# Second layer's first MLP product: four more f tiles as seven half-size products

## The chip, the cores and the metric

The kernel runs on one core of a Trainium2 chip. The metric is the time of one execution on the device, in microseconds (us); lower is better. All times here are of single-core runs of the whole program.

## What is computed

A decoder of two layers on one sequence of 512 tokens of 1024 columns, all in float32. The first layer mixes tokens by pooling windows, the second by a gated unit; each is followed by a norm, a modulation and an MLP with a squared ReLU. The change lies in the MLP of the second layer alone. Cut to that, the reference reads:

```python
def sq_relu_mlp(h, w1, w2):
    return jnp.square(jax.nn.relu(h @ w1)) @ w2

# for each layer i
h = modulate(rmsnorm(x, norm_mlp_g[i]), sh2, sc2)
x = x + g2[:, None, :] * sq_relu_mlp(h, mlp_w1[i], mlp_w2[i])
```

Here `h` is 512 x 1024, `mlp_w1[i]` is 1024 x 4096 and `mlp_w2[i]` is 4096 x 1024. The product with `w1` is called M1, the one with `w2` M2.

## The kernel before

**Three products for one.** Each float32 operand is split in two rounded parts, `h` and `l` ("high" and "low"): `split(r)` lets ACT copy the tile into `wh` (line 167) and DVE subtract it into `wl` (line 168); `parts(o, a)` does the same for activations (lines 592, 593). `mm3` (lines 176 to 178) then issues three matmuls for each product: `wl` by `h`, `wh` by `l`, `wh` by `h`. `H(k, c)` is the pair of parts of the normed activations (tile `hb`), for 128 input columns `k` and tokens `c`; `h32` holds the same values unsplit.

**M1 of the second layer.** The 4096 columns of `w1` are 32 tiles of 128, called f tiles; they are numbered in four chunks `c` of eight, and each chunk is two groups `j` of four. The result of a group is one tile `g[c, j]`.

- Tiles 0 to 3 of chunk 0 are made by `first1`: for each half of the tokens, four tiles of 8 times 3 matmuls of 256 columns. Between the halves the second half of the norm (`normed(1, 1, 1)`) runs, and `spill(1)` sends x out to memory.
- Tiles 4 to 7 of chunk 0 are the units `("f", (0, f))`: `f_prep` loads one weight tile (`w1f`, 512 KB) and splits it, `f_run` issues 2 x 8 x 3 = 48 matmuls of 256 columns, and `put` has ACT do the ReLU (line 630) and the square (line 618).
- Chunks 1 to 3 are units `("s", (c, j, m))`. A group of four f tiles by all the input columns is treated as a 2 x 2 block product and done as seven half-size products `m` after Winograd's scheme, in the order 1, 5, 6, 3, 7, 2, 4. Each has 2 x 4 x 3 = 24 matmuls of 256 columns. `s_prep` makes the weights of a product, `s_run` issues the matmuls and puts the results together: products 1, 6 and 5 are copied from the bank by ACT (line 742), 2, 3 and 7 are combined by DVE (lines 745, 747, 749), and each of the four blocks gets its ReLU (line 750) and its square.

**The weights of an s unit.** The four blocks `b(r, n)` of a group are loaded from `w1b` (512 KB each, SP queue, line 155) into the pool `w4`, which has three buffers. Block (0,0) is product 1's weight as it is; DVE then adds block (0,1) to it for product 5 and block (1,1) for product 6 (line 706), and after product 6's split a DMA on the POOL queue adds block (1,0) from memory for product 4 (line 701). A second such DMA adds block (1,1) to block (0,1) for product 7. Products 3 and 2 use blocks (1,1) and (1,0) as they are. Five pairs of `wh`, `wl` buffers (pool `wts`) let preparation run up to five units ahead of the matmuls.

**The activations of an s unit.** `a_sums(step)` makes the four operands that are sums, in steps 0 to 3 for products 5, 6, 3 and 7, out of `h32`, in place: one, one, two and no DVE operations of 128 x 1024 elements (lines 667 and 680 among them), and a `parts` each (one ACT, one DVE operation). Their results go to the tile of `hx`, to the buffers of `x0` and `x1` (free once x has been spilled), and to `H(slice(0, 4), half)`, over the activations that only plain products read. It is called after each of the four f units.

**The order of work.** TensorE (PE) runs in the order written. The other engines' instructions and the DMA issues are put in order when the program is built, by dependence and priority, and each engine then takes its queue in that order. M2 units `("p", (c, m))` follow from chunk 1 on, mixed with s units. `spread_cols(gain, dg)` (four matmuls, line 216) stands after the last unit of chunk 0.

Of the kernel before, what the change touches and what calls it, by code (L numbers as in the profile page):

```python
# [10 lines left out]
ALU = mybir.AluOpType  # L11
# [3 lines left out]
P = 128  # L15
D = 1024
# [29 lines left out]
def c_g(n, k):  # L46
    return 24 * n + 16 + k
# [31 lines left out]
def decoder_kernel(ctx: ExitStack, tc: tile.TileContext, xtok, vecs, rows, fgrow, ada0, adag, ada1, pool_w, w1s, w1, w1f, w1b, w2, w2e, w_v, w_u, w_o, wsT, lnp, bs, out):  # L79
    nc = tc.nc  # L80
    V, A, G, T = nc.vector, nc.scalar, nc.gpsimd, nc.tensor
# [13 lines left out]
    def shift(pool, words):  # L95

        if words % LINE:
            pool.tile([P, words % LINE], F32, name="shift", tag=f"shift{len(shifts)}", bufs=1)
            shifts.append(words)
# [6 lines left out]
    def bank(name, pool=None):  # L106
        pool = pool or ps
        return pool.tile([P, S], F32, name=name, tag="mm" if pool is ps else "xz")
# [33 lines left out]
    def H(k, c):  # L142

        return h_[0][:, 0, k, c], h_[0][:, 1, k, c]
# [8 lines left out]
    def raw4(src):  # L153
        r = w4.tile([P, D], F32, name="raw", tag="w4")
        nc.sync.dma_start(r, src)
        return r
# [7 lines left out]
    def split(r):  # L164

        h, l = wpair()
        A.activation(h, r, AF.Copy)  # L167
        V.tensor_tensor(l, r, f32(h), ALU.subtract)  # L168
        return h, l
# [35 lines left out]
    def diagonals(dg, cols):  # L205
        for k in range(KD):
            G.tensor_scalar(dg[:, k], ident, cols[:, k : k + 1], None, ALU.mult)

    def spread_cols(cols, dg=None):

        if dg is None:
            dg = w4.tile([P, KD, P], F32, name="dg", tag="w4")
            diagonals(dg, cols)
        for n in range(2):
            po = bank("pb")
            T.matmul(po, ones, dg[:, 4 * n : 4 * n + 4], start=True, stop=True)  # L216
            A.activation(gb[:, S * n : S * n + S], po, AF.Copy)
# [15 lines left out]
    with (  # L233
# [14 lines left out]
        m = band.rearrange("p n g w -> p (n g) w")  # L248
        G.affine_select(out=m, in_=m, compare_op=ALU.is_ge, fill=0.0, base=0, pattern=[[0, 8], [1, W]], channel_multiplier=-1)
        for g in range(4):  # L250
            m = band[:, :, g]
# [284 lines left out]
        for op in WORK.split():  # L536
            on_v, op = op.endswith("V"), op.rstrip("V")
            kind, d = op.rstrip("0123456789"), [int(c) for c in op if c.isdigit()]
# [51 lines left out]
    def parts(o, a):  # L590

        A.activation(o[0], a, AF.Copy)
        V.tensor_tensor(o[1], a, f32(o[0]), ALU.subtract)

    def mlp(i, first, extra, last, ending):
# [3 lines left out]
        with (  # L599
# [56 lines left out]
            def a_sums(step):  # L656


                def a(r, j):
                    return h32[0][:, 4 * j : 4 * j + 4, 256 * r : 256 * r + 256]  # L660

                def operand(pool, tag):
                    t = pool.tile([P, 2, 4, 256], F32R, name="as", tag=tag)
                    return t[:, 0], t[:, 1]

                def minus(o, p, q):
                    V.tensor_tensor(o, p, q, ALU.subtract)

                first, half = slice(0, 256), slice(256, 512)
                if step == 0:  # L670
                    sums_a.update({1: H(slice(0, 4), first), 2: H(slice(4, 8), first), 4: H(slice(4, 8), half)})
                    shift(hx, LINE - GAP)
                    minus(a(1, 1), a(1, 0), a(1, 1))
                    m, o = 5, operand(hx, "hx")
                elif step == 1:
                    minus(a(1, 1), a(1, 1), a(0, 0))
                    m, o = 6, operand(big, "x0")
                elif step == 2:
                    minus(a(0, 0), a(0, 0), a(1, 0))
                    V.tensor_tensor(a(1, 1), a(1, 1), a(0, 1), ALU.add)  # L680
                    m, o = 3, operand(big, "x1")
                else:
                    m, o = 7, H(slice(0, 4), half)
                parts(o, a(0, 0) if m == 7 else a(1, 1))
                sums_a[m] = o

            blks = {}

            def blk(c, j, r, n):
                if (c, j, r, n) not in blks:  # L690
                    blks[c, j, r, n] = raw4(w1b[2 * (c - 1) + j, r, n])
                return blks[c, j, r, n]

            def s_prep(u):
                c, j, m = u

                def b(r, n):
                    return blk(c, j, r, n)

                def add(o, r, n):  # L700
                    G.dma_start(o, w1b[2 * (c - 1) + j, r, n], accum_op=ALU.add)


                t = b(0, 0)
                if m in (5, 6):
                    V.tensor_tensor(t, t, b(*CHAIN[m]), ALU.add)
                if m == 5:
                    add(b(0, 1), 1, 1)
                wb = b(1, 1) if m == 3 else b(1, 0) if m == 2 else b(0, 1) if m == 7 else t
                w = split(wb)  # L710
                if m == 6:
                    add(t, *CHAIN[4])

                nxt = (c, j + 1) if j == 0 else (c + 1, 0)
                more = {1: (c, j, 0, 1), 5: (c, j, 1, 1), 3: (c, j, 1, 0), 7: (*nxt, 0, 0), 2: (*nxt, 0, 1), 4: (*nxt, 1, 1)}.get(m)
                if more and more[0] < 4:
                    blk(*more)
                return w
# [182 lines left out]
            gain = mods[i][:, c_g(1, 0) : c_g(1, 0) + KD]  # L901
            done = first(put)
            if i:
                dg = su.tile([P, KD, P], F32, name="dgu", tag="u")
                diagonals(dg, gain)
            units = [("f", (0, f)) for f in range(done, 8)]
            for c in range(3):
                if i == 0:
                    fs, lead, step = [("f", (c + 1, f)) for f in range(8)], 3, (1,) * 7
# [31 lines left out]
            for n, (kind, u) in enumerate(units):  # L941
                for m in range(n, ahead(n)):
                    if m not in ready:
                        ready[m] = prep[units[m][0]](units[m][1])
                while at < len(extra) and at < due * (n + 1):
                    extra[at]()
                    at += 1
                run[kind](u, ready[n])
                if i and kind == "f":
                    a_sums(u[1] - 4)  # L950
                    if u == (0, 7):
                        spread_cols(gain, dg)
                if i and u == (3, 1, 4):
                    reload()

# [77 lines left out]
    with (  # L1033
# [27 lines left out]
        for t in range(NT):  # L1061
# [6 lines left out]
            r = rsqrt(ag[:, 1:2], 1.0, LN_EPS, 1)  # L1068
# [4 lines left out]
        u, gt, wu = {}, {}, {}  # L1073
# [79 lines left out]
    def last1(t, c0, n, src, y):  # L1153
# [13 lines left out]
        else:  # L1167
# [5 lines left out]
            nc.sync.dma_start(out[t, :, 1], X(t)[:, S:D])  # L1173

    mlp(1, first1, [], last1, lambda: None)


# [11 lines left out]
def _lay_out(inp):  # L1189
    import numpy as np  # L1190

    def f(name):
        return np.asarray(inp[name], dtype=np.float32)

    def cols(v):
        return v.reshape(-1, P).T

    def fmajor(w, ct):

        return w.reshape(KD, P, -1, ct).transpose(2, 1, 0, 3).reshape(-1, P, KD * ct)  # L1200

    def halves(w):

        return w.reshape(4, 2, P, 2, S).transpose(3, 0, 2, 1, 4)

    order = _ada_columns()
    d = {}
    d["xtok"] = f("x")[0].reshape(NT, P, D)
    adab = f("ada_b").reshape(2, 48, P)[:, order]
    d["vecs"] = np.concatenate([cols(v) for v in (f("c"), adab, f("norm_mix_g"), f("norm_mlp_g"))], axis=1)  # L1210
    d["rows"] = np.stack([f("c")[0], adab[0, 16:24].reshape(-1), f("pool_scale")[0]])
    d["fgrow"] = f("final_g")
    aw = f("ada_w").reshape(2, D, 48, P)[:, :, order]

    v0 = aw[0].transpose(1, 2, 0)
    d["ada0"] = np.concatenate([v0[0:16], v0[24:40]] + [v0[16 + 2 * g : 18 + 2 * g] for g in GT])
    d["adag"] = aw[0][:, 16:24].reshape(2, 4, P, 4, 256).transpose(3, 0, 2, 1, 4)[GM]
    d["ada1"] = np.concatenate([v0[40:48], aw[1].transpose(1, 2, 0)])
    d["pool_w"] = f("pool_w")[0].reshape(8, P, 256).transpose(1, 0, 2)
    w1 = f("mlp_w1")  # L1220
    d["w1s"] = w1[0].reshape(KD, P, -1)[:, :, 0 : P * SWEEP]
    d["w1"] = fmajor(w1[0], P)
    d["w1f"] = fmajor(w1[1][:, :D], P)

    d["w1b"] = w1[1][:, D:].reshape(2, 4, P, 6, 2, 256).transpose(3, 0, 4, 2, 1, 5).reshape(6, 2, 2, P, D)

    w2 = f("mlp_w2").reshape(2, 4, 2, 4, P, 2, S)
    d["w2"] = w2[:, 0:3].transpose(0, 1, 2, 5, 4, 3, 6)
    d["w2e"] = np.stack([halves(w[3 * D :]) for w in f("mlp_w2")])
    win = f("sgu_w_in")[0]  # L1230
    d["w_v"] = halves(win[:, D:])
    d["w_u"] = fmajor(win[:, :D], P)
    d["w_o"] = halves(f("sgu_w_out")[0])
    d["wsT"] = f("sgu_w_s")[0].transpose(2, 0, 1)
    d["lnp"] = np.concatenate([f("sgu_ln_g")[0], f("sgu_ln_b")[0]])
    d["bs"] = f("sgu_b_s")[0].reshape(-1)
    return {k: np.ascontiguousarray(v) for k, v in d.items()}
# [17 lines left out]
```

## Time and profile before

| | us |
|---|---|
| median of 3 runs | 873.24 |
| lowest and highest | 872.81, 873.34 |
| the profiled execution, its own time | 873.16 |
| its span in the profile | 871.5 |
| granted TensorE clock, mean | 0.997 of full |

| engine | busy us | share of the span |
|---|---|---|
| TensorE matmul (PE) | 861.0 | 99% |
| weight load (PEld) | 741.6 | 85% |
| VectorE (DVE) | 670.1 | 77% |
| ScalarE (ACT) | 451.3 | 52% |
| GpSimd (POOL) | 66.9 | 8% |

Matmuls are pipelined: each is shown with its own length (0.28 us for 256 columns), but the next one starts well before it ends, so what a matmul costs is the distance from one start to the next. In the timeline a row gives the start, the length, the engine, the line, the operation, what is written and read, and in brackets the idle time of the engine just before it with what ended that.

### The profile page before, as it was taken

What the parts mean: (1) busy time and instruction counts of PE and PEld (TensorE: products, weight loads), DVE (VectorE), ACT (ScalarE), POOL (GpSimd) and SP (SyncE); (2) the same over time, 40 slices, a digit from 0 to 9 for tenths busy, and PEclk for the clock granted to TensorE, in tenths of its full rate; (3) what the DMA queues carried; (4) which work ended last, traced back from release to release, by engine and by line L of the source; (5) the groups of instructions that cost most, each with busy time, mean ns of one, the idle gap of its engine ahead of it and who ended that gap; (6) DMA issues with size and microseconds to landing.
All of it is one profiled execution on the core that took longest, in us unless ns stands there. A gap on an engine that the chain in (4) does not pass through costs nothing.

```text
span 871.5 us, 11804 instructions
## 1 busy us (share of the span) xinstructions
PE 861.0 (99%) x4580; PEld 741.6 (85%) x4580; DVE 670.1 (77%) x881; ACT 451.3 (52%) x653; POOL 66.9 (8%) x87
## 2 busy tenths in 40 slices
PE   9999999999999999999999999999999999999996
PEld 7878888788888888888878888999999998999885
DVE  6889696779869886657798866667777698679755
ACT  4285755554444445237333326666765576566521
POOL 3000003000000000000410012000101000100001
PEclk9999999999999999999999999999999999999998
DMA  9969853553554341615548525937758587677302
GB/s 350 417 229 311 274 193 137 193 193 121 181 204 169 128 162 51 215 37 205 193 155 288 185 73 222 319 87 179 171 193 178 156 225 224 136 162 261 123 24 97
DMA packets 39517, 161.80 MB, mean 186 GB/s; under 512 B 4387, under 2 KB 4515, under 8 KB 34214
## 3 DMA queue, kind: packets, MB, share of 16 engines
q1 hardware_dynamic: 35282, 137.72, 44.0%
q0 software_dynamic: 4032, 23.07, 13.0%
q8 instruction: 36, 0.59, 0.3%
q10 hardware_dynamic: 148, 0.27, 0.1%
q14 instruction: 19, 0.16, 0.1%
HBM read 156.84 MB, written 4.19 MB: 185 GB/s over the span
## 4 chain that ended last, share of the span: by engine, by line
PE 97%; ACT 2%; DVE 1%; issue 0%; POOLq 0%; POOL 0%; DVEq 0%; ACTq 0%
PE po L176 17%; PE po L178 17%; PE po L177 17%; PE pm L177 12%; PE pm L176 12%; PE pm L178 12%; PE pg L389 1%; PE pq L423 1%; PE po L1097 1%; PE po L437 1%; PE pg L288 1%; ACT sq L273 1%; PE px L992 1%; PE pb L216 1%; PE pc L288 1%; PE po L564 0%
## 5 line engine op out<-in xcount | busy, mean ns | idle before, releaser
L176 PE MATMUL po<-hb,wl 128*128 128x256 f32 (+1 forms) x624 | 209.5, 336 | 1.3 <-DVE wl L168 1.3
L178 PE MATMUL po<-hb,wh 128*128 128x256 f32 (+1 forms) x624 | 207.9, 333 | 0.0
L177 PE MATMUL po<-hb,wh 128*128 128x256 f32 (+1 forms) x624 | 207.8, 333 | 0.0
L168 DVE TENSOR_TENSOR wl<-raw,wh 128x1024 fp32r<-128x1024 f32 x107 | 130.9, 1224 | 45.6 <-ACT wh L167 45.3
L167 ACT ACTIVATE wh<-raw 128x1024 fp32r<-128x1024 f32 x107 | 112.7, 1057 | 63.1 <-PE pm L178 31.8
L176 PE MATMUL pm<-wh,ol 128*128 128x512 f32 x336 | 130.8, 389 | 0.0
L178 PE MATMUL pm<-wh,oh 128*128 128x512 f32 x336 | 130.8, 389 | 0.0
L177 PE MATMUL pm<-wl,oh 128*128 128x512 f32 x336 | 130.8, 389 | 0.0
L176 PEld LDWEIGHTS po<-hb,wl 128*128 128x128 f32 x624 | 117.2, 188 | 14.6 <-DVE wl L168 1.7
L177 PEld LDWEIGHTS po<-hb,wh 128*128 128x128 f32 x624 | 117.2, 188 | 12.9 <-issue 0.5
L178 PEld LDWEIGHTS po<-hb,wh 128*128 128x128 f32 x624 | 118.0, 189 | 11.8
L168 DVE TENSOR_TENSOR wl<-b,wh 128x1024 fp32r<-128x1024 f32 x60 | 72.8, 1222 | 26.0 <-ACT wh L167 26.0
L198 DVE SCALAR_TENSOR_TENSOR ada<-ada,cb 128x1024 f32<-128x1024 f32 x56 | 68.4, 1222 | 16.6 <-DMA ada<-in_ada 16.4
L178 PEld LDWEIGHTS pm<-wh,oh 128*128 128x128 f32 x336 | 63.1, 188 | 13.1
L176 PEld LDWEIGHTS pm<-wh,ol 128*128 128x128 f32 x336 | 63.1, 188 | 12.3
L177 PEld LDWEIGHTS pm<-wl,oh 128*128 128x128 f32 x336 | 63.1, 188 | 12.2
L167 ACT ACTIVATE wh<-b 128x1024 fp32r<-128x1024 f32 x60 | 63.4, 1056 | 17.5 <-PE pm L178 9.1
L630 ACT ACTIVATE g<-po 128x512 f32<-128x512 f32 x40 | 23.6, 599 | 75.4 <-PE po L178 73.9
L168 DVE TENSOR_TENSOR wl<-bt,wh 128x1024 fp32r<-128x1024 f32 x24 | 29.1, 1223 | 28.8 <-ACT wh L167 28.8
L969 ACT ACTIVATE tmp<-x 128x512 f32<-128x512 f32 (+1 forms) x25 | 15.3, 612 | 66.0 <-DVE x L965 66.0
L857 DVE TENSOR_TENSOR y<-y,pm 128x512 f32<-128x512 f32 x68 | 43.7, 682 | 1.0 <-PE pm L178 1.0
L177 PE MATMUL po<-as,wh 128*128 128x256 f32 x144 | 40.5, 281 | 0.0
(211 smaller groups left out, 1494.7 us busy)
## 6 DMA issues: line engine op xcount, KB each, us to landing
ada<-in_ada SPq DMA_DIRECT2D x72, 512.0 KB, 3.3
b<-in_w SPq DMA_DIRECT2D x21, 1024.0 KB, 4.9
raw<-in_w SPq DMA_DIRECT2D x25, 512.0 KB, 3.7
raw<-in_w1b SPq DMA_DIRECT2D x24, 512.0 KB, 4.7
bt<-in_w POOLq DMA_DIRECT2D x9, 1024.0 KB, 8.0
raw<-in_w2e SPq DMA_DIRECT2D x16, 512.0 KB, 3.2
raw<-in_w1b POOLq DMA_DIRECT2D x12, 512.0 KB, 5.3
wh<-in_ada SPq DMA_DIRECT2D x9, 512.0 KB, 9.6
```

The lines of the kernel that those rows point to most:

```text
L167: A.activation(h, r, AF.Copy)
L168: V.tensor_tensor(l, r, f32(h), ALU.subtract)
L176: T.matmul(o, wl, mh, start=first, stop=False, **kw)
L177: T.matmul(o, wh, ml, start=False, stop=False, **kw)
L178: T.matmul(o, wh, mh, start=False, stop=last, **kw)
L198: V.scalar_tensor_tensor(r, r, 1.0, cb, ALU.mult, ALU.mult, accum_out=pmv[i, b][:, j : j + 1])
L216: T.matmul(po, ones, dg[:, 4 * n : 4 * n + 4], start=True, stop=True)
L273: A.activation(j, X(t)[:, c], AF.Square, scale=D**-0.5, accum_out=out)
L288: T.matmul(o[:, 0:n], ones, what[:, 0:n], start=True, stop=True)
L630: A.activation(t, po, AF.Relu)
L857: V.tensor_tensor(yt, yt, banks[hf], ALU.subtract if minus else ALU.add)
L969: A.activation(tmp, xt, AF.Square, scale=D**-0.5, accum_out=s[:, len(cs) : len(cs) + 1])
```

## The change

Tiles 4 to 7 of chunk 0 become one more group of seven half-size products: units `("s", (0, 1, m))` in the order 1, 2, 5, 6, 3, 7, 4, product 2 standing second here. `w1b` grows by this group (seven groups instead of six, so its index moves by one), and `w1f` keeps only the four tiles of `first1`. The steps of `a_sums` are now called in `s_prep`, ahead of the weights of products 5, 6, 3 and 7, and no longer after the runs of the f units. For this group the blocks are loaded in the order (0,0), (1,0), (0,1), (1,1), where the other groups load (0,0), (0,1), (1,1), (1,0); block (0,0) of the next group is asked for after product 7 as elsewhere, block (0,1) of it after product 4 rather than after product 2, and block (1,1) of it after that group's product 5. `spread_cols` stands behind product 4.

```diff
-                    blks[c, j, r, n] = raw4(w1b[2 * (c - 1) + j, r, n])
+                    blks[c, j, r, n] = raw4(w1b[2 * c + j - 1, r, n])
...
-                    G.dma_start(o, w1b[2 * (c - 1) + j, r, n], accum_op=ALU.add)
+                    G.dma_start(o, w1b[2 * c + j - 1, r, n], accum_op=ALU.add)
+
+                if c == 0 and m in (5, 6, 3, 7):
+                    a_sums((5, 6, 3, 7).index(m))
...
-                more = {1: (c, j, 0, 1), 5: (c, j, 1, 1), 3: (c, j, 1, 0), 7: (*nxt, 0, 0), 2: (*nxt, 0, 1), 4: (*nxt, 1, 1)}.get(m)
+                more = {5: (c, j, 1, 1), 7: (*nxt, 0, 0), 4: (*nxt, 0, 1)}
+                more |= {1: (c, j, 1, 0), 2: (c, j, 0, 1)} if c == 0 else {1: (c, j, 0, 1), 3: (c, j, 1, 0), 2: (*nxt, 0, 1), 4: (*nxt, 1, 1)}
+                more = more.get(m)
...
-            units = [("f", (0, f)) for f in range(done, 8)]
+
+            units = [("s", (0, 1, m)) for m in (1, 2, 5, 6, 3, 7, 4)] if i else [("f", (0, f)) for f in range(done, 8)]
...
-                if i and kind == "f":
-                    a_sums(u[1] - 4)
-                    if u == (0, 7):
-                        spread_cols(gain, dg)
+                if i and u == (0, 1, 4):
+                    spread_cols(gain, dg)
...
-    d["w1f"] = fmajor(w1[1][:, :D], P)
+    d["w1f"] = fmajor(w1[1][:, : D // 2], P)
...
-    d["w1b"] = w1[1][:, D:].reshape(2, 4, P, 6, 2, 256).transpose(3, 0, 4, 2, 1, 5).reshape(6, 2, 2, P, D)
+    d["w1b"] = w1[1][:, D // 2 :].reshape(2, 4, P, 7, 2, 256).transpose(3, 0, 4, 2, 1, 5).reshape(7, 2, 2, P, D)
```

## The prediction

> **What bounds the kernel now.** I read the page first: span, engine shares, the chain that ended last.
>
> ```profile
> span 871.5 us, 11804 instructions
> PE 861.0 (99%) x4580; PEld 741.6 (85%) x4580; DVE 670.1 (77%) x881; ACT 451.3 (52%) x653; POOL 66.9 (8%) x87
> PE 97%; ACT 2%; DVE 1%; issue 0%; POOLq 0%; POOL 0%; DVEq 0%; ACTq 0%
> ```
>
> TensorE is busy 99% of the span and makes 97% of the chain. So the time falls by what is taken off TensorE's own stream, as long as nothing makes it wait. Next the stretches around the change. The columns after each window are its length, then busy time (and instruction count) of PE, PEld, DVE, ACT, POOL, then granted clock, share of the DMA engines, GB/s.
>
> ```profile
> 540.00:548.00 8.00, 7.92 (x69) 7.92 (x70) 4.93 (x7) 4.50 (x6) 2.19 (x4) 1.00 0.94 331
> 548.00:556.00 8.00, 8.00 (x73) 8.00 (x72) 5.72 (x9) 4.01 (x8) 0.34 (x1) 1.00 1.00 414
> 556.00:563.73 7.73, 7.73 (x70) 7.73 (x69) 6.18 (x6) 7.31 (x10) 0.60 (x1) 1.00 0.93 212
> 563.73:585.50 21.77, 21.77 (x195) 21.77 (x194) 13.84 (x13) 12.81 (x18) 1.70 (x2) 1.00 0.51 132
> ```
>
> The last row is the stretch that the change rewrites (the four f units). PE never idles in it, the clock is full, DVE is busy 64% and ACT 59%. The DMA engines are full until 563.7 and half idle after.
>
> **Term 1: the matmuls.** The change takes out 4 x 48 = 192 matmuls and puts in 7 x 24 = 168, all of 256 columns. I price each kind by the distance of starts, from TensorE's timeline. The first pair of rows bounds the 192 f matmuls, the second pair 72 matmuls of three s units that stand back to back.
>
> ```profile
> 563.73 0.28 PE L176 MATMUL po<-hb,wl 128*128 128x256 f32 x1
> ...
> 585.50 0.59 PE L216 MATMUL pb<-dgu,ones 128*128 128x512 f32 x1
> ...
> 664.86 0.28 PE L176 MATMUL po<-hb,wl 128*128 128x256 f32 x1
> ...
> 673.34 0.39 PE L176 MATMUL pm<-wh,ol 128*128 128x512 f32 x1
> ```
>
> The f kind costs 21.77 / 192 = 0.1134 us, the s kind (673.34 - 664.86) / 72 = 0.1178 us, 4% more for the same shape. So the new stretch takes 168 x 0.1178 = 19.79 us, and the gain is 21.77 - 19.79 = 1.98 us. At the f kind's price it would be 24 x 0.1134 = 2.72 us. I take 1.98, because the units that come in are s units in every respect (same tiles, same slices of them). The Trainium skill, "TensorE: Matmul & The Clock Gate", sections on the back-to-back issue gap and on LDWEIGHTS, would make the spacing the same for both kinds: it prices a weight load by its 128 columns (about 107 ns) and a warm matmul by its 256 (about 109 ns), and by that the gain would be some 2.6 us. The two pairs of rows differ where that rule sees no difference, so here the trace speaks against it.
>
> **Term 2: the work beside it.** Each new unit needs its weight split; products 5 and 6 need a DVE addition of blocks; three results are copied by ACT and three combined by DVE. The prices:
>
> ```profile
> L168 DVE TENSOR_TENSOR wl<-raw,wh 128x1024 fp32r<-128x1024 f32 x5 | 6.1, 1223 | 2.3 <-ACT wh L167 2.3
> L706 DVE TENSOR_TENSOR raw<-raw 128x1024 f32<-128x1024 f32 x2 | 2.5, 1225 | 0.1
> L593 DVE TENSOR_TENSOR as<-h,as 128x1024 fp32r<-128x1024 f32 x2 | 2.4, 1222 | 0.0
> L168 DVE TENSOR_TENSOR wl<-bt,wh 128x1024 fp32r<-128x1024 f32 x1 | 1.2, 1227 | 3.2 <-ACT wh L167 3.2
> L680 DVE TENSOR_TENSOR h<-h 128x1024 f32<-128x1024 f32 x1 | 1.2, 1221 | 0.0
> L593 DVE TENSOR_TENSOR ol<-g,oh 128x1024 fp32r<-128x1024 f32 x1 | 1.2, 1217 | 0.0
> L167 ACT ACTIVATE wh<-raw 128x1024 fp32r<-128x1024 f32 x4 | 4.2, 1060 | 2.9 <-DMA raw<-in_w1f 2.0 <-DVE raw L706 0.9
> L742 ACT ACTIVATE g<-po x18: 581/598/601, 590.6 to 792.7; 128x512 f32<-128x512 f32 x18
> L747 DVE TENSOR_TENSOR g<-po,g x6: 684/686/692, 605.2 to 795.6; 128x512 f32<-128x512 f32 x6
> ```
>
> Added on DVE: 3 more splits (3.67), 2 additions (2.45), 3 combinations (2.06; lines 745 and 749 taken at line 747's price), 8.2 us. Added on ACT: 3 x 1.06 + 3 x 0.60 = 5.0 us. ReLUs, squares and the steps of `a_sums` stay as many. DVE already does work in this stretch that isn't due in it: three splits and two additions for chunk 1, the split of `bt` and the `ol` for M2, 3 x 1.22 + 2 x 1.22 + 1.23 + 1.22 = 8.6 us. What is due is then 13.84 - 8.6 + 8.2 = 13.4 us in 19.8 (68%). Average load hides it at no cost; what can cost is order and latency.
>
> **Term 3: two chains of weights.** With s units of 24 x 0.1178 = 2.83 us from 563.73 on, the products start at 563.7 (1), 566.6 (2), 569.4 (5), 572.2 (6), 575.0 (3), 577.9 (7), 580.7 (4), and the block ends at 583.5. `w4` has three buffers: (0,0) and (0,1) are held until products 4 and 7, so block (1,1) can be asked for only when product 2's split has freed (1,0)'s. Loads and splits as they fell for tiles 4 to 7:
>
> ```profile
> 556.42 1.06 ACT L167 ACTIVATE wh<-raw 128x1024 fp32r<-128x1024 f32 x1 [2.83 <-DMA raw<-in_w1f]
> 565.78 1.06 ACT L167 ACTIVATE wh<-raw 128x1024 fp32r<-128x1024 f32 x1 [2.01 <-DMA raw<-in_w1f]
> 561.05 1.22 DVE L168 TENSOR_TENSOR wl<-raw,wh 128x1024 fp32r<-128x1024 f32 x1
> 558.76 0.33 SPq L155 DMA_DIRECT2D raw<-in_w1f  x1
> raw<-in_w1f SPq DMA_DIRECT2D x1, 512.0 KB, 7.0
> 562.30 0.33 SPq L155 DMA_DIRECT2D raw<-in_w1b  x1
> raw<-in_w1b SPq DMA_DIRECT2D x1, 512.0 KB, 4.7
> L701 POOL DMA_DIRECT2D raw<-in_w1b x12: 847/848/857, 572.3 to 785.9; - x12
> DMA to landing us min/median/max: 5.1/5.3/5.9
> ```
>
> The first four loads take the places of those for f tiles 4 to 7. The split of the second of them began on DVE at 561.05, ended at 562.27, and SP issued the next load at 562.30: that is where block (1,1) goes. It landed 4.7 us later, the load issued at 558.76 took 7.0. So block (1,1) is there at 567.0, or at 569.3 by the slow row. Then addition, ACT half and DVE half, 1.22 + 1.06 + 1.22 = 3.5 us: product 6's weight is ready at 570.5, or 572.8. It is due at 572.2: 1.7 us to spare, or 0.6 us of stall. I take 4.7 us, the row of that moment and the same state of the DMA engines, so no stall.
>
> Product 4 hangs on product 6's split: then POOL's accumulating DMA (line 701, 5.1 to 5.9 us from issue to landing), then 1.06 + 1.22. From 570.5 that gives 570.5 + 5.3 + 2.28 = 578.1, from 572.8 at most 581.0, against 580.7 (581.3 if product 6 is 0.6 late): no stall. POOL's queue holds the accumulation for product 7 before it, issued after product 5's addition, before 565; nothing else there is due. Product 7 and product 3 have their blocks from 570 on. On SP's queue nothing that waits for a buffer holds back another transfer that is due: what follows are the raw blocks of chunk 1.
>
> `a_sums` now stands in the preparation. Its step 0 already ran at 554 to 560 beside `first1`, and steps 1 and 2 before they were due, so this adds no work, only a due time: step 2 (two additions, an ACT half, a DVE half, 4.7 us) must be done by 575.0. Step 3 overwrites the second-half activations of `hb` while products 1, 2 and 4 read other parts of that tile. That such parts are told apart is visible: PE read first halves without a gap (the row 548 to 556, PE 8.00 of 8.00) while the norm wrote second halves of `hb` there.
>
> **After the block** chunk 1 starts with less prepared. Its block (1,1) gets a buffer only when product 4's split is done (578.1 to 581.0): 4.7 + 3.5 us later is 586.3 to 589.2, due two units and four `pb` matmuls after 583.5, so after 583.5 + 5.7 = 589.2. It holds, with little to spare in the late case. The four `pb` matmuls of `spread_cols` move with the end of the block and cost the same.
>
> **Sum:** 873.16 (the profiled execution's own time) - 1.98 + 0 = 871.18; the median of the runs is 0.08 above that execution. I forecast 871.2 us. 0.2% of this time, about what a measurement of this kernel can tell from no change, is 1.75 us: the limit is at 871.5, so the gain clears it by 0.2 us only.
>
> **The rivals.**
>
> *The new units run at the f units' spacing* (the page's rule above): 873.16 - 2.72 = 870.4. For it: the operands lie in the same pools. Against it: every s unit I looked at has 0.1178. Chance 0.07.
>
> *Product 6 comes late, by one or two transfers and queue places* (no measurable change). If block (1,1) needs 7.0 us, 0.6 us is lost; if besides it one or two DVE operations of 1.22 us stand ahead in the queue, 1.8 to 3.0. That gives 871.8 to 874.2. For it: 1.7 us is not much, the new block asks two accumulating DMAs more of the DMA engines, and both ACT rows above waited for a load (2.83 and 2.01 us) with work behind them. Chance 0.25.
>
> *DVE's queue is blocked behind a late block* (slower than before). The order of the queues is fixed when the program is built. If the addition of block (1,1) stands ahead of the rest of steps 1 and 2, a late load delays them all. Say it lands at 570.5 (8.2 us, one DVE operation beyond the slow row): addition to 571.7, step 1's DVE half to 572.9, product 6's half to 574.1, so PE is 1.9 late; step 2's two operations to 576.5, ACT half 577.6, DVE half 578.8, product 3's half 580.0, when it is due at 575.0 + 1.9: 3.1 more. In all 5.0 us, so 871.2 + 5.0 = 876.2. It decides against the change once the stalls pass 1.98 + 1.75 = 3.7 us. For it: those ACT waits on loads with a queue behind. Against it: the two additions of line 706 had 0.1 us of idle time before them, so there the queue's order fitted the landings. Chance 0.27.
>
> That the change doesn't take work off TensorE can't be: 24 matmuls go, whatever the queues do.
>
> **How the numbers follow.** The forecast, with stalls below 0.25 us and 870.9 to 871.5 as its own range, gets 0.41. Faster by over 0.2%: 0.41 + 0.07 = 0.48; within 0.2%: 0.25; slower: 0.27. The range goes from 870.4 (the f spacing) to 876.2 (the blocked queue) and leaves out about 0.13 above and 0.02 below.
>
> **What would show it.** PE should have 4556 matmuls, the seven units should take 19.8 us from the end of `first1` to the `pb` matmuls, with starts 0.118 apart: 0.113 would speak for the first rival. PE idle time before product 6 or 4, put down to `wl`, with DVE waiting on ACT or on a load of `w1b`, would show the second; a gap before product 3 with DVE's step 2 operations behind the addition, the third. PE idle time in chunk 1 that was not there before would show that the lost lead is not covered. I am wrong if the block is gap-free and the time is still above 871.5.

## The result and the profile after

| | before | changed |
|---|---|---|
| median, us | 873.29 (4 runs) | 881.11 (4 runs) |
| lowest and highest | 872.81, 873.37 | 878.35, 881.93 |
| the profiled execution, its span | 873.16, 871.5 | 878.35, 876.6 |

The changed kernel takes 1.0084 times as long, 95% interval 1.0071 to 1.0097. Its page, the same three lines as before:

```profile
span 876.6 us, 11779 instructions
PE 857.8 (98%) x4556; PEld 738.8 (84%) x4556; DVE 677.0 (77%) x889; ACT 456.3 (52%) x659; POOL 69.1 (8%) x89
PE 32%; DMA 2%; issue 1%; DVE 1%; ACT 1%; POOL 0%; POOLq 0%; DVEq 0%; ACTq 0%
```

The 24 matmuls are gone (4580 to 4556) and PE is busy 3.2 us less, yet the span is 5.1 us longer. So PE waits. (The chain of the third line is followed here over less than half of the span, so its shares can't be set beside those of before.) The waits of PE from 500 us on (waiting line, what released it, us in total, times, longest):

```profile
PE po L176 <- ACT g L747: 4.8, 1, 4.8
PE po L176 <- DVE wl L168: 1.2, 1, 1.2
PE po L176 <- DVE g L754: 1.1, 1, 1.1
```

The middle one was there before the change (1.3 us, at the start of `first1`). The other two are new and not waits for weights: lines 747 and 754 (742 and 749 before) take results out of PSUM banks. PE's timeline, from the first matmul of the block to the `pb` matmuls:

```profile
563.20 0.28 PE L176 MATMUL po<-hb,wl 128*128 128x256 f32 x1
...
579.36 0.39 PE L176 MATMUL po<-as,wl 128*128 128x256 f32 x1 [4.81 <-ACT g L747]
...
587.82 0.38 PE L176 MATMUL po<-hb,wl 128*128 128x256 f32 x1 [1.12 <-DVE g L754]
...
590.66 0.59 PE L216 MATMUL pb<-dgu,ones 128*128 128x512 f32 x1
```

The block takes 590.66 - 563.20 = 27.46 us where the four f tiles took 21.77. Product 3 waits 4.81 us, product 4 1.12 us. What ACT, POOL and DVE did at those moments:

```profile
571.63 0.85 POOL L701 DMA_DIRECT2D raw<-in_w1b  x1 [10.03 <-DVE wl L168]
572.25 1.05 ACT L592 ACTIVATE oh<-g 128x1024 fp32r<-128x1024 f32 x1
577.25 1.06 ACT L167 ACTIVATE wh<-raw 128x1024 fp32r<-128x1024 f32 x1 [3.95 <-DMA raw<-in_w1b]
578.21 0.61 ACT L755 ACTIVATE g<-g 128x512 f32<-128x512 f32 x1
578.73 0.58 ACT L747 ACTIVATE g<-po 128x512 f32<-128x512 f32 x1
587.08 0.68 DVE L754 TENSOR_TENSOR g<-g,po 128x512 f32<-128x512 f32 x1
```

At 571.63 POOL issues the accumulating DMA for product 4's weight. From 573.3 to 577.25 ACT stands at that weight's split. Behind it in ACT's queue is the copy of product 5 (578.73), and product 3 adds into the bank which that copy empties. So a weight that is due two units later holds up the unit that is next. At 587.08 DVE combines product 7 out of the bank into which product 4, now directly behind product 7, adds.

The gap has a second price, in the granted clock (the column after POOL's) of the stretch behind it:

```profile
576.00:579.36 3.36, 0.00 (x1) 0.00 (x1) 1.50 (x2) 2.11 (x4) 0.00 (x0) 1.00 0.91 319
579.36:583.00 3.64, 3.64 (x18) 3.64 (x19) 2.36 (x3) 1.90 (x3) 0.00 (x0) 0.54 0.44 151
```

Until the start at 583.12 the matmuls are 0.21 us apart: 18 of them in 3.76 us where 18 x 0.1134 = 2.04 would do, 1.7 us lost. Together: 168 x 0.1134 = 19.05, gaps 5.93 and clock 1.7 make 26.7. The other 0.8 of the 27.46 is what is left: the wider distances of starts at each gap, and product 6 at 0.118 us a matmul.

### The profile page after: what moved, and what is told of

Read it like the earlier page. It is cut to its first block, busy times and chain, and to the rows that moved or that the text cites. A ratio compares the mean times of both kernels' runs of the same rounds, so it can differ in the third digit from the quotient of the medians.

```text
span 876.6 us, 11779 instructions
## 1 busy us (share of the span) xinstructions
PE 857.8 (98%) x4556; PEld 738.8 (84%) x4556; DVE 677.0 (77%) x889; ACT 456.3 (52%) x659; POOL 69.1 (8%) x89
## 3 DMA queue, kind: packets, MB, share of 16 engines
q0 software_dynamic: 4320, 24.12, 13.6%
## 5 line engine op out<-in xcount | busy, mean ns | idle before, releaser
L176 PE MATMUL po<-hb,wl 128*128 128x512 f32 (+1 forms) x592 | 200.7, 339 | 2.3 <-DVE wl L168 1.2
L177 PE MATMUL po<-hb,wh 128*128 128x512 f32 (+1 forms) x592 | 198.9, 336 | 0.0
L178 PE MATMUL po<-hb,wh 128*128 128x512 f32 (+1 forms) x592 | 198.9, 336 | 0.0
L168 DVE TENSOR_TENSOR wl<-raw,wh 128x1024 fp32r<-128x1024 f32 x110 | 134.4, 1223 | 46.8 <-ACT wh L167 46.6
L167 ACT ACTIVATE wh<-raw 128x1024 fp32r<-128x1024 f32 x110 | 115.8, 1056 | 67.7 <-PE pm L178 31.8
L176 PEld LDWEIGHTS po<-hb,wl 128*128 128x128 f32 x592 | 111.2, 188 | 15.8 <-DVE wl L168 1.6
L177 PEld LDWEIGHTS po<-hb,wh 128*128 128x128 f32 x592 | 111.2, 188 | 13.0 <-issue 0.5
L178 PEld LDWEIGHTS po<-hb,wh 128*128 128x128 f32 x592 | 112.0, 189 | 11.8
L630 ACT ACTIVATE g<-po 128x512 f32<-128x512 f32 x36 | 21.2, 599 | 72.2 <-PE po L178 70.5
L176 PE MATMUL po<-as,wl 128*128 128x256 f32 x168 | 48.1, 286 | 4.8 <-ACT g L747 4.8
L178 PE MATMUL po<-as,wh 128*128 128x256 f32 x168 | 47.9, 285 | 0.0
```

Source lines behind the costliest of these rows:

```text
L176: T.matmul(o, wl, mh, start=first, stop=False, **kw)
L177: T.matmul(o, wh, ml, start=False, stop=False, **kw)
L178: T.matmul(o, wh, mh, start=False, stop=last, **kw)
L630: A.activation(t, po, AF.Relu)
```

## The experiments

All times are medians beside runs of the kernel before on the same chip (873.3 to 873.7 there).

**e1: the late split behind the copies.** In `s_prep`, for products (0,1,4) and (1,0,1), whose preparation is also held back to after the run of product 6:

```diff
-                w = split(wb)
+                    with tc.issue_after(copied[0, 1, 6].ins):
+                        w = split(wb)
```

> The changed kernel, with one edit: ACT's half of the weight splits of product 4 and of the next group's product 1 is queued behind ACT's copy of product 6 (in the changed kernel product 4's stood ahead of the copy of product 5). Theory (the queue): product 3 waited 4.81 us because ACT stood 3.95 us at product 4's split, which waits for the accumulating DMA, with the copy that frees product 5's bank behind it; the matmuls after the gap then ran at a granted clock of 0.54. So the gap before product 3 and the clock drop go, the gap of 1.1 us before product 4 (DVE's combination of product 7 out of the same bank) stays, the block is 20.7 to 21.0 us long and the time about 872.2. Rival (late weights or too much work on DVE and ACT): the weights come no earlier, so the gap moves to product 4 or 3 and PE idles 4 us or more in the block; time above 876.

Measured: 879.3 us (877.0 to 881.4), ratio 1.0060 (1.0043 to 1.0077). The rival's number. But look at what stood first:

```profile
570.43 1.23 DVE L711 TENSOR_TENSOR raw<-raw 128x1024 f32<-128x1024 f32 x1 [4.77 <-DMA raw<-in_w1b]
571.69 2.00 ACT L167 ACTIVATE wh<-raw 128x1024 fp32r<-128x1024 f32 x2 [4.87 <-DVE raw L711]
574.55 0.57 ACT L753 ACTIVATE g<-po 128x512 f32<-128x512 f32 x1
575.21 0.55 PE L176 MATMUL po<-as,wl 128*128 128x256 f32 x1 [3.61 <-ACT g L753]
```

Here block (1,1), issued at 561.14, landed after 9.2 us and not after 5.3 as in the changed kernel's profile. DVE stood 4.77 us at its addition, ACT as long at the split behind it, and the copy of product 1 (574.55) came so late that product 6 waited 3.61 us for the bank. The gap before product 3, at which the edit aimed, shrank from 4.81 to 0.70; product 4 waited 1.84. So the edit did what it should and the next late transfer took its place: the queue alone doesn't settle it.

**e2: no accumulation for product 4.** In `s_prep`:

```diff
-                if m == 6:
+                if m == 6 and u != (0, 1, 6):
```

> The changed kernel without the accumulating DMA for product 4 of the new group: its weight lacks block (1,0), everything else and the order of ACT's queue are the same. Theory (the queue): ACT no longer stands at product 4's split, so the copy of product 5 comes in time; the 4.81 us gap and the clock drop go although no instruction of ACT or DVE is moved, the 1.1 us before product 4 stays; about 872. Rival (late block (1,1), or the load of ACT and DVE): nothing that product 3 waits for has changed, 878 to 882 as before.

Measured: 881.2 us (879.8 to 883.3), ratio 1.0092 (1.0073 to 1.0110). PE's waits behind 500 us:

```profile
PE po L176 <- DVE g L754: 3.2, 1, 3.2
PE po L176 <- ACT g L747: 1.8, 2, 1.3
```

With ACT's order unchanged, taking away the DMA it stood at brought the gap before product 3 from 4.81 to 1.30. That part of the theory held; block (1,1) took 5.5 us here as in the changed kernel's first profile, so the late block is not what shortened the gap. The total did not fall, and the time is the rival's: product 4 now waited 3.2 us. Product 7's matmuls ended at 583.2, but DVE came to its combination (line 754) only behind the split for chunk 1's product 5 and the addition for its product 6:

```profile
583.32 1.23 DVE L168 TENSOR_TENSOR wl<-raw,wh 128x1024 fp32r<-128x1024 f32 x1 [0.53 <-ACT wh L167]
584.58 1.22 DVE L709 TENSOR_TENSOR raw<-raw 128x1024 f32<-128x1024 f32 x1
585.72 0.68 DVE L754 TENSOR_TENSOR g<-g,po 128x512 f32<-128x512 f32 x1
```

**e3: the `pb` matmuls before product 4.** `spread_cols` at unit (0,1,7) instead of (0,1,4).

> The changed kernel with the four pb matmuls (1.3 us) moved to between products 7 and 4. Theory (the bank): product 4 adds into the bank that DVE reads for product 7, so it must wait for that reading; with 1.3 us of other matmuls between, the 1.12 us gap before it goes, and the 4.81 us gap and the clock drop stay: 1.1 us less than the changed kernel, 877 to 881. Rival (product 4 waits for its weight): the gap stays behind the pb matmuls or before them, no gain.

Measured: 879.2 us (877.8 to 879.9), ratio 1.0059 (1.0043 to 1.0074). The wait for line 754 is gone and the one for line 747 stays (4.64 us before product 3, another 1.57 before product 6; block (1,1) took 7.5 us here). As expected for this gap. The runs spread by 2 us, so the 1.1 us itself can't be read from the times.

**e4: both.** e1 and e3 together.

> Both edits: the splits behind ACT's copy of product 6, and the pb matmuls between products 7 and 4. Theory: no gap in the block, 19.65 us (two products at 2.72, five at 2.84), against 21.77 for the four f tiles: about 871.2, 2.1 us below the kernel before. Rival (late weights): a gap before product 4, since its weight hangs on product 6's split, the accumulating DMA and a split; 872 to 874.

Measured: 878.3 us (877.3 to 881.5), ratio 1.0058 (1.0041 to 1.0075). The theory's 871.2 was wrong, and so were the rival's 872 to 874. In the profile, of the slowest of the six runs, block (1,1) took 9.2 us again, DVE stood 4.79 us at it, and products 6 and 3 waited 2.58 and 1.99 us. Two waits of 0.76 and 1.04 us came in chunk 1. So the late block was tried next.

**e5: the blocks early.** Blocks (1,0) and (1,1) go into a buffer that waits for M2's blocks until then (in `blk`, asked for with product 1):

```diff
+                    if c == 0 and r == 1:
+                        if n == 0:
+                            pair.append(w2p.tile([P, 4, S], F32, name="b", tag="b", bufs=2))
+                        o = pair[0][:, 2 * n : 2 * n + 2].rearrange("p a b -> p (a b)")
+                        nc.sync.dma_start(o, w1b[2 * c + j - 1, r, n])
```

> The changed kernel with blocks (1,0) and (1,1) of the new group loaded into one of the two 8 KB buffers of M2's blocks (tag b), free at that time, so that they don't wait for a buffer of w4; M2's own transfers into that buffer come later. Nothing else is moved by hand. Theory (late loads): what ACT's and DVE's queues stood at was block (1,1), asked for at 561 and there at 566.6 to 571, and the accumulation that hangs on its split; with it there by 560 the gaps before products 6, 3 and 7 go and about 1.1 us before product 4 stays: 872 to 873. Rival (too much work on DVE and ACT between 554 and 585): the work is the same, PE idles 3 us or more: above 876.

Measured: 877.7 us (877.1 to 878.4), ratio 1.0048 (1.0033 to 1.0063). That is the rival's number, and PE idles 3.9 us in the block as the rival said; whether work is the reason is left to e7. Products 1, 2, 5 and 6 now follow each other without a gap. What is left is the first theory's wait: ACT at product 4's split (below), so product 3 starts 2.70 us late, with 1.19 us before product 4 and half the clock behind the first.

```profile
575.57 1.06 ACT L167 ACTIVATE wh<-raw 128x1024 fp32r<-128x1024 f32 x1 [4.03 <-DMA raw<-in_w1b]
```

**e6: early blocks and both moves.**

> The early blocks together with the two edits tried before (product 4's split behind ACT's copy of product 6, pb matmuls before product 4). Theory (late loads, then the bank): no gap in the block, 871 to 872, below the kernel before. Rival (work): gaps of 2 us or more stay, above 875.

Measured: 875.6 us (874.5 to 878.4), ratio 1.0030 (1.0017 to 1.0043). Above the theory and at the rival's number, but not for the rival's reason: in its profile, of the slowest of the seven runs, the block is nearly clean (one gap of 0.52 us) and takes 20.0 us without the `pb` matmuls. The time is lost later, in the stretch of chunk 1, where of the kernels so far only e4 had waited. The first and the last of PE's five waits there (4.2 us together), and ACT before the first of them:

```profile
605.94 2.00 ACT L167 ACTIVATE wh<-bt 128x1024 fp32r<-128x1024 f32 x2 [9.84 <-DMA bt<-in_w]
607.05 0.49 PE L176 MATMUL pm<-wh,ol 128*128 128x512 f32 x1 [0.58 <-ACT wh L167]
...
631.14 0.36 PE L176 MATMUL po<-as,wl 128*128 128x256 f32 x1 [1.09 <-DVE wl L168]
```

M2's weight `bt` is a chain: split, accumulating DMA, split. In the kernel before its first split began at 580.7, in the middle of the f tiles and 15.0 us before its unit; here at 589.3. The DMA that hangs on it was issued 5.4 us later than there (594.2 against 588.8) and took 11.8 us to land instead of 7.9, with another accumulating DMA (590.7 to 597.7) in the same time: it landed at 605.9 instead of 596.7.

**e7: no operand sums.** `a_sums` is not called; `sums_a` holds plain parts of `H`.

> The changed kernel without the steps of a_sums: products 5, 6, 3 and 7 of every group read plain activations instead of their sums, so eight DVE operations (9.8 us) and four on ACT (4.2 us) are left out between 554 and 576, while the loads stay as they are. Rival (work): the gaps go, 873 or less. Theory (late loads): ACT still stands at product 4's split and the queues at block (1,1); only what was behind that block in DVE's queue gets shorter, so PE idles 3 us or more: 876 to 878.

Measured: 882.5 us (881.3 to 882.8), ratio 1.0105 (1.0088 to 1.0122). Both ranges were missed. The block, though, took 27.2 us, as in the changed kernel (27.5): fourteen us of work less on two engines, and not faster:

```profile
570.59 1.23 DVE L711 TENSOR_TENSOR raw<-raw 128x1024 f32<-128x1024 f32 x1 [6.51 <-DMA raw<-in_w1b]
```

DVE stands idle 6.51 us for block (1,1), which took 9.1 us to land in this run. PE idles 5.7 us in the block, so it isn't the amount of work on DVE or ACT that makes PE wait there. The loss beyond the changed kernel lies ahead of the block: the wait at the start of `first1` was 2.73 us instead of 1.23, with half the clock behind it, some 3 us together. Why this edit lengthens that wait was not looked into.

**e8: product 2 late again.** The one part of the change undone: the order 1, 5, 6, 3, 7, 2, 4 and the other groups' order of loads.

> The changed kernel with one part undone: the new group's products in the order of the others (1, 5, 6, 3, 7, 2, 4) and its blocks loaded in their order, so (1,1) third and (1,0) only when product 3's split has freed a buffer. Theory (late loads and the bank): block (1,1) comes with the first loads, by 560, and product 2 stands between 7 and 4, so the 1.1 us before 4 and most of the gap before 3 go; product 2's block is the late one now, and may cost 1 to 2 us: 872 to 875. Rival (work): 877 to 881, as changed.

Measured: 877.2 us (877.0 to 878.2), ratio 1.0045 (1.0030 to 1.0060). That is the rival's number, above the theory's 872 to 875. Yet the block did as the theory said: 20.97 us, 0.8 less than the f tiles and 6.5 less than the changed kernel's block, with waits of 0.45 and 0.19 us. With nothing else moved, the order of the other groups is the better one here; e6 shows that the new order can do with less still (20.0 us) once its blocks come early. But chunk 1 loses 2.8 us at places like those of e6:

```profile
619.16 0.49 PE L176 MATMUL pm<-wh,ol 128*128 128x512 f32 x1 [0.96 <-ACT wh L167]
620.42 0.50 PE L177 MATMUL pm<-wl,oh 128*128 128x512 f32 x1 [0.77 <-DVE wl L168]
629.85 0.36 PE L176 MATMUL po<-as,wl 128*128 128x256 f32 x1 [1.08 <-DVE wl L168]
```

**e9: M2's first sums on DVE.** e6, and for chunk 0 M2's products 5 and 6 add loaded blocks by DVE (the first layer's branch), so two accumulating DMAs of 1 MB leave the chain. Product 7's sum, a third such DMA, goes to DVE with them, which the expectation doesn't count: the queue of accumulating DMAs moves 3.15 MB less than in the changed kernel (20.97 against 24.12).

```diff
+                by = by_dma and c > 0
...
-                    if not by_dma:
+                    if not by:
...
-                    nxt = {1: 5, 5: 6, 6: 4}.get(m)
+                    nxt = ({1: 5, 5: 6, 6: 4} if by else {6: 4}).get(m)
...
-                    if m == 3:
+                    if m == 3 and by:
```

> The kernel with the early blocks and the two moves, and besides for chunk 0 M2's first two sums of blocks (products 5 and 6) made by DVE from loaded blocks rather than by accumulating DMAs into bt (two DMAs of 1 MB less, two DVE operations of 2.4 us more). In the run without this, the block was nearly free of gaps, but PE then idled 4.2 us between 607 and 632, at M2 products whose weight waited for bt's accumulation. Theory (lost lead: the f tiles' stretch was where ACT, DVE and the DMA queues got ahead of PE, and what waits first after it is bt's chain): with that chain cut, those gaps go: 871 to 872.5. Rival (the stretch after the block has too much work on DVE): the gaps come back at other waits, 875 or more.

Measured: 871.85 us (870.6 to 872.7, 11 runs) against 873.51, ratio 0.9974 (0.9965 to 0.9983): faster than both kernels. Behind 500 us PE has one wait left, the old one. Its block:

```profile
563.35 0.28 PE L176 MATMUL po<-hb,wl 128*128 128x256 f32 x1
...
579.95 0.59 PE L216 MATMUL pb<-dgu,ones 128*128 128x512 f32 x1
581.54 0.41 PE L176 MATMUL po<-hb,wl 128*128 128x256 f32 x1
...
584.50 0.28 PE L176 MATMUL po<-hb,wl 128*128 128x256 f32 x1
```

584.50 - 563.35 - (581.54 - 579.95) = 19.56 us against 21.77. So once every wait is covered the block gains 2.2 us, between the 1.98 and the 2.72 that the count of matmuls gives at the two prices; the medians differ by 1.7. Shorter chain or less load on the DMA engines: this edit does both, and no run parts them.

**e10 and e11.** The same M2 edit on e8, and on the kernel before.

> The kernel with the order 1, 5, 6, 3, 7, 2, 4 and the loads in their order (block 20.97 us, then 2.8 us of gaps at M2's weights), with the same edit of M2's sums. The accumulation of 1 MB that filled the DMA engines from 555 to 564 goes too. Theory: the gaps after the block go, the block stays at 21: 872 to 873. Rival: 875 to 877, as without.

> The control: the kernel before with the same edit of M2's sums alone. PE had no gap after 540 in the kernel before, so there is nothing to gain: both theories say no change, 873.2, unless DVE's two more operations make a gap (up to 876).

Measured: e10 874.4 us (873.6 to 875.3), ratio 1.0004 (0.9995 to 1.0013), 2.8 us below e8 but above its expectation; its profile has waits of 0.54 and 0.46 us in the block (21.1 us) and none in chunk 1. e11 873.2 us, ratio 0.9996 (0.9986 to 1.0006): no change. So the M2 edit gains nothing by itself; it repairs what the new block breaks.

**r1: the changed kernel again.**

> The changed kernel once more, on the chip of the others: 878 to 882, gaps before products 3 and 4 of the new group (4 to 5 and 1 us) and matmuls at half clock after the first of them.

Measured: 880.8 us (879.9 to 881.3), ratio 1.0076 (1.0061 to 1.0091). The same two gaps (4.68 and 1.00 us). By the `pb` matmuls this profile is 2.5 us behind the first one: 0.6 were lost ahead of `first1`, about 1 us because the matmuls from `first1` to product 6 ran at 0.1178 us and not at 0.1134, and 0.8 because the half clock lasts 6.8 us here and not 3.4.

## Why the prediction was wrong

The forecast was 871.2 with a range to 876.2. Step by step:

- **Term 1, the matmuls.** Right in count, a little off in price. In the first profile products 1, 2 and 5 ran at 0.1134 us (2.72 us each), not at 0.1178; in r1 the same products ran at 0.1178. At 0.1134 throughout the gain would have been 2.7, the first rival's number. So the price is not one of f or s units: the reason given ("s units in every respect") was wrong, and the two pairs of rows did not show that the kinds differ. The last section has what the profiles show of the two prices.
- **Term 2, the work beside it.** The average was right: e7 takes 14 us of it away and the block stays as long.
- **Term 3 is the step that failed.** It followed two chains of weights to their due times and found both in time: in the changed kernel they were (product 6's split ended at 571.3, due 571.5). It looked only at when a weight is ready and not at what stands behind it in an in-order queue while it isn't. Two waits follow from that. The split of product 4 was done at 579.6, in time by the forecast's 580.7, and ACT stood before it with product 5's copy behind: product 3 waited 4.81 us, and 1.7 more went in clock. Where the forecast had no stall, this step alone is more than three times the gain it forecast. And the change's second half was not followed into PSUM: product 4 adds into product 7's bank, with no unit between since product 2 was moved: 1.12 us.
- **Block (1,1).** Its landing time was taken from one row (4.7 us, 7.0 at most). It took 5.3 to 9.2 us in the seven profiles in which it is asked for behind product 2's split (changed, r1, e1 to e4, e7), beside two accumulating DMAs: M2's of 1 MB, at 555.0 to 563.8 in the changed kernel, and product 7's, at 560.8 to 567.9. That the first of them lengthens loads is seen in e11, where it is left out of the kernel before: the two loads from which the prediction took 7.0 and 4.7 us landed in 4.0 and 3.2. With 9.2 the second and third rival's mechanism is there (e1, e4), at the place named but with another victim: copies behind it on ACT, not product 3's operand on DVE.
- **"After the block"** was called safe by 0 to 2.9 us for chunk 1's block (1,1). M2's chain through `bt` was counted only as work that "isn't due". e6 and e8 show it was the one that breaks next, and e9 that cutting it gives the gain back. In the f tiles' stretch ACT and DVE had one split to make per 5.44 us of matmuls, in the new one per 2.8: losing the lead that this built cost 4.2 and 2.8 us of waits in e6 and e8, more than the 24 matmuls bring.
- **The third rival** (slower, a late block with a queue behind it) was the nearest: right in kind, wrong in engine, place and size (876.2 against 881).

What is shown: the wait at the queue by e2, which moves nothing and shortens it from 4.81 to 1.30 us (e1 brings it to 0.70, but there product 6 came 3.6 us late and left ACT more time), the wait at the bank by e3, the one for the block by e5, and the lost lead by e6, e8, e9, e10 and e11. What is not: which of the edits in e9 could be left out, whether its M2 edit helps by the shorter chain or by the fewer DMAs, and why block (1,1) lands in 5.3 us in one run and 9.2 in another.

## What to carry to other kernels

For every instruction that will wait, ask not only whether it is in time but what stands behind it on its engine, and whether one of those frees a bank or buffer that the bound engine needs next. When cheaper matmuls replace a stretch in which the other engines got ahead, price the lead: follow the longest chain of the next stretch back to where its first link used to run. Products that add into a shared bank need another unit between them at least as long as the reading of the bank, the time that the reading stands in its engine's queue included.

## What the runs showed of the hardware

**The same matmul at two paces.** Matmuls of 256 columns ran at 0.1134 or at 0.1178 us, each for long stretches, and not by their kind. Product 1 in e2 (first pair of rows, 2.82 us for 24) and product 5 in e5 (second pair, 2.72 us):

```profile
563.98 0.28 PE L176 MATMUL po<-hb,wl 128*128 128x256 f32 x1
566.80 0.28 PE L176 MATMUL po<-hb,wl 128*128 128x256 f32 x1
...
569.38 0.28 PE L176 MATMUL po<-as,wl 128*128 128x256 f32 x1
572.10 0.28 PE L176 MATMUL po<-as,wl 128*128 128x256 f32 x1
```

The pace changed only where the stream was interrupted: at a wait, be it a start held back by 0.1 us, or at matmuls of another shape. In e2, e4, e8, e10 and r1 `first1` ran at the slow pace, in the other nine profiles at the fast one. A stretch of 384 such matmuls (540 to 585 in the kernel before) is 1.7 us longer at the slow pace, as much as the medians of some of these kernels differ by. What sets the pace was not tried.

**The clock goes by windows of 3.41 us, not by gaps.** The granted clock was at half behind a gap of 1.84 us (e1, before product 4) and behind 1.99 (e4, before product 3), but at full behind 2.58 (e4, before product 6). The traces record when the clock changes. Within each of the 14 profiles all changes lie whole multiples of 3.41 us apart, so each execution has its own grid of windows. The second column below is the length of a window, the third the time that PE was busy in it, the one after POOL's the clock. The first pair is e1's gap of 1.84 us, the others are e4's gaps of 2.58 and 1.99 us:

```profile
584.96:588.37 3.41, 1.57 (x14) 1.37 (x13) 2.83 (x5) 2.25 (x4) 0.65 (x1) 1.00 0.33 130
588.37:591.79 3.42, 3.42 (x18) 3.42 (x18) 2.44 (x2) 1.96 (x3) 0.20 (x1) 0.50 0.75 116
...
571.67:575.08 3.41, 1.65 (x15) 1.44 (x13) 3.41 (x4) 2.70 (x3) 0.00 (x0) 1.00 0.01 2
575.08:578.49 3.41, 2.59 (x22) 2.62 (x23) 3.41 (x4) 2.63 (x4) 0.85 (x1) 1.00 0.31 25
578.49:581.91 3.42, 1.43 (x12) 1.22 (x12) 2.40 (x3) 2.12 (x5) 0.00 (x0) 1.00 0.99 235
581.91:585.32 3.41, 3.41 (x19) 3.41 (x18) 1.23 (x1) 1.99 (x2) 0.00 (x0) 0.50 0.56 213
```

The gap of 2.58 us lay across two windows, 1.76 us idle in one and 0.8 in the other, and the clock stayed. Of all windows at full clock from 20 us on, in the 14 profiles, each with 1.84 us or more of idle PE was followed by half the clock and none with 1.76 or less, so the limit here lies at about half a window. (Ahead of that, at 7.6 us of e5, the clock halved once behind a window that shows PE busy; this stays open.) The clock came back at the end of a half-clock window that had at most 0.49 us of idle PE, and stayed at half with 0.64 (e2) and 1.42 (r1). So what a gap of 2 to 3.5 us costs depends on where in the grid it falls, and a gap that costs clock costs up to 1.7 us per window. The Trainium skill, "TensorE: Matmul & The Clock Gate", section on the HAM clock gate, has the clock halve after an idle window of some 3.4 us that runs on its own, whatever the kernel does. The window's length and its running on its own agree with these rows; it need not be idle throughout, over half was enough here.
